# A two-layer network with a gated mixing layer: another order of the mixing steps, and down products held back by two blocks

## The chip, the cores and the metric

The kernel runs on one core of a Trainium2 chip. The core has a matrix engine (TensorE, PE in the profile, with its weight loads PEld), a vector engine (VectorE, DVE), an activation engine (ScalarE, ACT), a general engine (GpSimd, POOL) and a queue engine that issues most of the transfers (SyncE, SP). Each engine works through its own stream of instructions; semaphores between the streams carry the dependences. The metric is the device time of one execution in microseconds (us); less is better.

## The reference

The input is 256 tokens of 1024 features. The network has a gated delta-rule layer, a feed-forward, a sliding-window attention layer, a second feed-forward, then a mixing layer and a layer of selected experts. The change touches the two feed-forwards and the mixing layer:

```
def conv_gated_mlp(hn, w_up, conv_w, conv_b, w_down):
    u = causal_dwconv(hn @ w_up, conv_w, conv_b)
    gate, val = jnp.split(u, 2, axis=-1)
    return (jax.nn.silu(gate) * val) @ w_down
```

```
h = rmsnorm_2(x, norm1_g[l])
z = h @ w_in[l]
conv_in = z[..., :o_conv]                                  # 2048 wide
q, k, v = ...                                              # 16 query heads, 4 key and value heads
gates = jax.nn.sigmoid(z[..., o_v:]).reshape(b, s, 2, d)   # 2 x 1024
conv_out = conformer_conv(conv_in, ...)
attn_out = windowed_gqa(q, k, v, attn_sink[l]) @ attn_w_o[l]
merged = gates[:, :, 0, :] * conv_out + gates[:, :, 1, :] * attn_out
x = x + merged @ w_out[l]
```

`conformer_conv` gates one half of its input with the sigmoid of the other, runs a 31-tap depthwise convolution over the tokens, a layer norm over the 1024 channels, SiLU, and a pointwise product. The feed-forward is 2816 wide on each side; its convolution has 3 taps.

## The kernel before

Activations lie transposed: 128 features on the partitions, 256 tokens along the free axis, so 1024 features are eight blocks. Every large product is made of three matmuls (`mm3`, L237 to L241): a float32 weight is split into a high part `wh` (cast on ScalarE, L232) and a low remainder `wl` (VectorE or GpSimd, L223), the activation likewise into `xh` and `xl`, and wh·xh + wh·xl + wl·xh is summed in PSUM. `proj` (L247) makes 256 output columns from 1024 inputs with 48 such matmuls and two weight pieces of half a megabyte; `kouter` (L262) adds the share of two input blocks to all eight output blocks, also 48 matmuls and two pieces. Pieces go through pools of four buffers.

PSUM is eight banks in three pools: `pp` (2), `pm` (2) and `pa` (4). A product that adds over a whole stage (`acc4`) holds all four `pa` banks. While `self.wide` is set, projections go round over `pp` and `pa`.

**Feed-forward** (`ffn`, L749): a loop over 11 blocks of 256 columns. Each makes two projections (gate and value), evicts and convolves them on VectorE and ScalarE, multiplies, and splits the result into `gh` (L788) and `gl` (L789). `lower` adds the block's down product to the four `pa` banks. It is held back in `pend`, so that block i's down product is written behind block i+1's projections; the last one follows the one before it.

**Mixing** (`mix`, L1290): steps are functions, and the string `MIX` (L75) says in which order they are written. A step is a letter and a number:
- `c0..c3` convolution input: two projections, sigmoid, product, into the padded tile `upad`;
- `d0..d15` convolution: block m = i // 2, first or second half of the 31 taps. ScalarE makes the first tap (L1326), VectorE adds each further one in a dependent step (L1329); the running sum of two blocks at a time lies in one `pm` bank (`taps`), the last tap goes to the tile `conv`;
- `q`, `k` projections for the heads; `S0..S7`, `P0..P7` scores and values of one key head and one block of queries;
- `g0..g7` gate projections (L1345), of which 0 to 3 are the first branch's (convolution) and 4 to 7 the second's (attention); `s` their sigmoid;
- `o0..o3` the attention's output product (transposes at L1218, low halves at L1224, then `kouter` into the `pa` banks); `a0` multiplies it with the second branch's gates (L1355);
- `L0` the layer norm's mean (column sums of `conv`, L319; a row over all partitions, L299) and subtraction (L1365); `N0` its variance, scaling and SiLU (L1373 to L1384); `R0` a scaling of the residual;
- `w0..w3` pointwise products with the gates, `e0..e3` the layer's output product.

The string is the order in which the program is written. A scheduler then places the instructions of each engine, before the kernel runs, by a timeline of its own; it keeps the order in which tiles of a pool are handed out. So a tile of `pm` is given to a later step only when an earlier one has released it: `taps` holds one of the two banks until the convolution is over, and column sums, rows and the transposes of `o` share the other.

Of the kernel before, what the change touches and what calls it, by code (L numbers as in the profile page):

```python
# [11 lines left out]
F32R = mybir.dt.float32r  # L12
# [9 lines left out]
P = 128  # L22
T = 256
# [15 lines left out]
def shape_constants():  # L39
# [7 lines left out]
    for k in range(DB):  # L47
# [24 lines left out]

GDN = "d0 d1 d2 z0 p0 d3 p1 p2 p3 b0 v1 v0 z1 i0 s1 v2 s0 z2 i2 o1 v3 o0 s2 z3 s3 o2 o3"
SWA = "q2 q0 S0 S1 P0 q1 S3 S2 P1 S4 P3 o0 P2 P4 q3 S5 o1 S7 P7 S6 P5 P6 o2 o3"
MIX = ("c0 q0 d0 d1 q1 d2 c1 d3 k0 d4 S0 S1 d5 P0 q2 d6 P1 S2 c2 d7 S3 P2 d8 q3 P3 d9 S4 c3 d10 S5 P4 d11 g4 S6 d12 "  # L75
       "P5 g5 S7 d13 P6 g6 d14 P7 g7 d15 s8 s12 o0 o1 o2 o3 a0 g0 g1 L0 g2 g3 N0 R0 s0 s4 w0 w1 e0 w2 e1 w3 e2 e3")
PEER = " ".join([f"q{i} k{i}" for i in range(8)] + [f"T{i}" for i in range(8)] + [f"u{i}" for i in range(32)])


# [8 lines left out]
class Net:  # L88
# [21 lines left out]
    def t(self, pool, shape, tag, dt=F32, **kw):  # L110
        return pool.tile(shape, dt, tag=tag, name=self.nm(tag), **kw)
# [637 lines left out]
    def ffn(self, l, nxt, hook=None, each=None):  # L749
        nc, tc, I, t = self.nc, self.tc, self.I, self.t  # L750
        up, down = I["ffn_w_up"][l], I["ffn_w_down"][l]
        cw, cb = self.fconv[l], self.fbias[l]
        self.stage = "ffn"
        x = self.input(self.v["ffn_norm_w"][:, 8 * l : 8 * l + 8])
        with tc.tile_pool(name=f"ffn{l}", bufs=2) as fp:
            _, rrow = self.rstd(self.hT, fp, "sq")
            acc = None
            pend = []
            self.wide, self.nwide = True, NW[0]

            def lower(i, gh, gl):
                nonlocal acc
                if acc is None:
                    acc = self.acc4()
                self.kouter(acc, down, (2 * i, 2 * i + 1), [(gh[:, kk, :], gl[:, kk, :]) for kk in range(2)],
                            i == 0, i == 10)

            for i in range(11):
                if hook:
                    hook(i)  # L770
                cv = []
                for part in range(2):
                    ps = self.proj(up, part * 2816 + 256 * i, x)
                    nc.vector.tensor_mul(ps, ps, self.bc(rrow))
                    o = t(fp, [P, 2, T], f"cv{part}")
                    for m in range(2):
                        blk = part * 22 + 2 * i + m
                        w = [cw[j][:, blk : blk + 1] for j in range(3)]
                        nc.scalar.activation(o[:, m, :], ps[:, m, :], AF.Identity, scale=w[2], bias=cb[:, blk : blk + 1])
                        for d in range(1, 3):  # L780
                            nc.vector.scalar_tensor_tensor(o[:, m, d:], ps[:, m, : T - d], w[2 - d], o[:, m, d:],
                                                           op0=ALU.mult, op1=ALU.add)
                    cv.append(o)
                nc.scalar.activation(cv[0], cv[0], AF.Silu)
                nc.vector.tensor_mul(cv[0], cv[0], cv[1])
                gh = t(fp, [P, 2, T], "gh", F32R, bufs=3)
                gl = t(fp, [P, 2, T], "gl", F32R, bufs=3)
                nc.scalar.copy(gh, cv[0])  # L788
                nc.vector.tensor_sub(gl, cv[0], gh.bitcast(F32))  # L789
                pend.append((i, gh, gl))  # L790
                if len(pend) > 1:
                    lower(*pend.pop(0))
            lower(*pend.pop(0))
            self.residual(acc, nxt, None, each)


# [493 lines left out]
    def mix(self):  # L1290
# [5 lines left out]
        with tc.tile_pool(name="mix", bufs=1, reuse_waits="tile") as mp, \  # L1296
# [106 lines left out]
            def resnorm(_):  # L1403

                row = self.rrow(r1, ap, "sc256")
                for k in range(DB):
# [3 lines left out]
            self.wide, self.nwide = True, NW[3]  # L1410
            self.play(MIX, c=conv_in, d=conv, k=lambda _: self.heads_kv(w_in, 3072, 3328, x, rrow, rcol, kT, v),
                      q=lambda i: self.heads_q(w_in, 2048, x, rrow, qT, i, self.c[:, C_SL : C_SL + DB]), g=gate, s=sig,
# [82 lines left out]
```

## Time and profile before

| | |
|---|---|
| median of three runs | 2007.62 us (2006.73 to 2009.07) |
| the profiled execution | 2006.97 us, of which the span from first to last instruction is 2005.2 us |
| delta-rule layer | 0 to 324 us |
| first feed-forward | 324 to 510 us |
| window attention | 510 to 609 us |
| second feed-forward | 609 to 803 us |
| mixing, to its last output product | 803 to 1071 us |
| experts and end | to 2005.2 us |
| HBM read, written | 298.60 MB, 4.74 MB: 151 GB/s over the span |
| main transfer queue | 49.2% of the 16 DMA engines' time |

Times in the profile are microseconds from the first instruction, durations in the group rows are nanoseconds. "L1329" is a line of the kernel; `pm<-upad,colsdw,pm` names the tile written and those read. What stands in brackets is the time that the engine sat idle ahead of the row, and what ended it. The granted clock is TensorE's, as a share of full speed.

### The profile page before, as it was taken

The numbers are of one execution on the slowest core, as the hardware profiler recorded it, in microseconds if no ns is written. First come the engines' busy times: TensorE is split into PE (matmuls) and PEld (weight loads), VectorE is DVE, ScalarE is ACT, GpSimd is POOL, SyncE is SP. The second block draws the span as 40 slices with busy tenths as digits, with TensorE's granted clock in tenths as the row PEclk, the third lists the DMA queues.
The fourth block names the chain that finished last, engine by engine and source line by source line (L and its number), as shares of the span: only waits on it lengthen the run. The fifth ranks groups of instructions, "written<-read, shape, count | busy, mean of one in ns | idle before, by whom it ended". The sixth has DMA issues, their size and how long they took to land. (4 is left out here: it accounts for less than half of the span.)

```text
span 2005.2 us, 36808 instructions
## 1 busy us (share of the span) xinstructions
PE 1867.5 (93%) x14537; PEld 1760.0 (88%) x14537; DVE 1464.4 (73%) x2685; ACT 958.3 (48%) x1419; POOL 709.2 (35%) x325
## 2 busy tenths in 40 slices
PE   7879999999899999999969988799999999999998
PEld 7879999999889999989969978699989978887886
DVE  6786656766536666688854899977999977886555
ACT  5744435555555555556445434234333334344443
POOL 5444343544323444755634445454332300000000
PEclk9989999999899999999979999999999999999999
DMA  6454236566424665433535544456455545445555
GB/s 201 124 146 139 89 100 202 190 191 195 126 83 147 202 191 176 153 121 117 162 102 150 147 128 138 119 159 174 137 147 138 148 147 167 159 160 172 194 194 173
DMA packets 243434, 306.29 MB, mean 153 GB/s; under 512 B 26076, under 2 KB 213821, under 8 KB 243133
## 3 DMA queue, kind: packets, MB, share of 16 engines
q1 hardware_dynamic: 240864, 302.84, 49.2%
q8 instruction: 114, 1.87, 0.4%
q10 hardware_dynamic: 2237, 1.07, 0.2%
q14 instruction: 59, 0.48, 0.1%
q0 software_dynamic: 160, 0.02, 0.0%
HBM read 298.60 MB, written 4.74 MB: 151 GB/s over the span
## 5 line engine op out<-in xcount | busy, mean ns | idle before, releaser
L223 POOL TENSOR_TENSOR wl<-raw,wh 128x1024 fp32r<-128x1024 f32 (+1 forms) x196 | 470.7, 2405 | 555.0 <-ACT wh L232 506.9
L232 ACT CAST wh<-raw 128x1024 fp32r<-128x1024 f32 (+1 forms) x285 | 297.8, 1048 | 322.2 <-issue 108.9
L239 PE MATMUL pa<-xh,wh 128*128 128x256 f32 (+1 forms) x1336 | 388.8, 291 | 26.9 <-ACT wh L981 17.8
L239 PE MATMUL pp<-xh,wh 128*128 128x256 f32 x1392 | 395.5, 284 | 16.6 <-DVE kq L481 9.8
L241 PE MATMUL pp<-xh,wl 128*128 128x256 f32 x1392 | 394.3, 283 | 4.1 <-DVE wl L223 2.6
L241 PE MATMUL pa<-xh,wl 128*128 128x256 f32 (+1 forms) x1336 | 386.8, 291 | 11.0 <-DVE wl L223 7.6
L240 PE MATMUL pp<-xl,wh 128*128 128x256 f32 x1392 | 393.1, 282 | 2.1 <-DVE xl L364 2.1
L240 PE MATMUL pa<-xl,wh 128*128 128x256 f32 (+1 forms) x1336 | 385.3, 289 | 1.6 <-DVE xl L364 1.5
L223 DVE TENSOR_TENSOR wl<-raw,wh 128x1024 fp32r<-128x1024 f32 x233 | 296.8, 1274 | 112.3 <-ACT wh L232 55.8
L223 POOL TENSOR_TENSOR wl<-rt,wh 128x1024 fp32r<-128x1024 f32 x80 | 203.2, 2546 | 272.4 <-ACT wh L981 258.9
L239 PEld LDWEIGHTS pa<-xh,wh 128*128 128x128 f32 (+1 forms) x1336 | 262.3, 197 | 32.2 <-ACT wh L981 21.6
L239 PEld LDWEIGHTS pp<-xh,wh 128*128 128x128 f32 x1392 | 266.9, 192 | 18.8 <-issue 10.2
L241 PEld LDWEIGHTS pa<-xh,wl 128*128 128x128 f32 (+1 forms) x1336 | 262.1, 197 | 13.7 <-DVE wl L223 8.7
L241 PEld LDWEIGHTS pp<-xh,wl 128*128 128x128 f32 x1392 | 266.8, 192 | 6.1 <-DVE wl L223 3.7
L240 PEld LDWEIGHTS pp<-xl,wh 128*128 128x128 f32 x1392 | 267.1, 192 | 2.5 <-DVE xl L364 2.3
L240 PEld LDWEIGHTS pa<-xl,wh 128*128 128x128 f32 (+1 forms) x1336 | 262.1, 196 | 3.0 <-DVE xl L364 1.9
L981 ACT CAST wh<-rt 128x1024 fp32r<-128x1024 f32 x128 | 133.9, 1049 | 223.1 <-DVE rt L978 204.3
L1086 PE MATMUL pa<-wh,rt 128*128 128x512 f32 x512 | 200.9, 394 | 0.0
L1085 PE MATMUL pa<-wl,rt 128*128 128x512 f32 x512 | 200.3, 391 | 0.0
L1076 ACT CAST wh<-raw 128x1024 fp32r<-128x1024 f32 x128 | 134.5, 1051 | 108.6 <-PE pa L1086 97.3
L978 DVE STREAM_TRANSPOSE rt<-raw 128x1024 f32<-128x1024 f32 x128 | 156.3, 1229 | 16.9 <-POOL wl L223 16.6
L1084 PE MATMUL pa<-wh,rt 128*128 128x512 f32 x512 | 161.4, 393 | 1.4 <-ACT rt L1070 1.4
(422 smaller groups left out, 3450.2 us busy)
## 6 DMA issues: line engine op xcount, KB each, us to landing
raw<-in_peer_u_dram SPq DMA_DIRECT2D x512, 128.0 KB
raw<-in_peer_v_dram SPq DMA_DIRECT2D x128, 512.0 KB
raw<-in_ffn_w_up_dram SPq DMA_DIRECT2D x88, 512.0 KB
raw<-in_a_w_in_dram SPq DMA_DIRECT2D x48, 512.0 KB
raw<-in_ffn_w_down_dram SPq DMA_DIRECT2D x44, 512.0 KB
raw<-in_w_in_dram SPq DMA_DIRECT2D x44, 512.0 KB
raw<-in_a_w_out_dram SPq DMA_DIRECT2D x16, 512.0 KB
raw<-in_peer_w_query_dram SPq DMA_DIRECT2D x16, 512.0 KB
```

The costliest lines, as they stand in the source:

```text
L223: (self.nc.vector if order[self.turn % len(order)] == "D" else self.nc.gpsimd).tensor_tensor(out, raw, high, op=ALU.subtract)
L232: nc.scalar.copy(wh, raw)
L239: mm(out, wh, xh, start=start, stop=False, skip_group_check=skip)
L240: mm(out, wh, xl, start=False, stop=False, skip_group_check=skip)
L241: mm(out, wl, xh, start=False, stop=stop, skip_group_check=skip)
L978: nc.vector.transpose(rt, raw)
L981: nc.scalar.copy(uh.rearrange("p f (b e) -> p f b e", b=4), rv)
L1076: nc.scalar.copy(vh, raw)
L1084: nc.tensor.matmul(o, w2[:, 0, i, s], vh[:, c], start=first, stop=False)
L1085: nc.tensor.matmul(o, w2[:, 0, i, s], vl[:, c], start=False, stop=False)
L1086: nc.tensor.matmul(o, w2[:, 1, i, s], vh[:, c], start=False, stop=last)
```

## The change

The string for mixing gets another order, and the feed-forward keeps two blocks' results in `pend` instead of one, with four buffers for `gh` and `gl` instead of three.

```diff
-MIX = ("c0 q0 d0 d1 q1 d2 c1 d3 k0 d4 S0 S1 d5 P0 q2 d6 P1 S2 c2 d7 S3 P2 d8 q3 P3 d9 S4 c3 d10 S5 P4 d11 g4 S6 d12 "
-       "P5 g5 S7 d13 P6 g6 d14 P7 g7 d15 s8 s12 o0 o1 o2 o3 a0 g0 g1 L0 g2 g3 N0 R0 s0 s4 w0 w1 e0 w2 e1 w3 e2 e3")
+MIX = ("c0 q0 d0 q1 d1 k0 d2 c1 d3 S0 d4 S1 q2 d5 P0 d6 c2 S2 d7 P1 d8 S3 q3 d9 c3 d10 P2 S4 d11 P3 d12 S5 d13 "
+       "P4 S6 d14 P5 d15 S7 P6 g4 P7 g5 L0 g6 g7 s8 s12 o0 o1 o2 N0 o3 a0 g0 g1 R0 g2 g3 s0 s4 w0 w1 e0 w2 e1 w3 e2 e3")
...
-                gh = t(fp, [P, 2, T], "gh", F32R, bufs=3)
-                gl = t(fp, [P, 2, T], "gl", F32R, bufs=3)
+                gh = t(fp, [P, 2, T], "gh", F32R, bufs=4)
+                gl = t(fp, [P, 2, T], "gl", F32R, bufs=4)
...
-                if len(pend) > 1:
+                if len(pend) > 2:
                     lower(*pend.pop(0))
-            lower(*pend.pop(0))
+            for p in pend:
+                lower(*p)
```

Behind L792 the changed kernel's lines have a number higher by one. What the scheduler makes of the change is seen in each engine's stream. Three places of it follow, as rows of line, operation, tile written and tiles read, size, and how often the row stands there in succession.

TensorE at the end of the second feed-forward, before: the last row of block 10's value projection (`pp`), then the down product of block 9 (48 matmuls, the first one shown) and that of block 10.

```order
L241 MATMUL pp_9065<-xh_6951,wl_9100 128x256
L239 MATMUL pa_7300<-gh_8932,wh_9142 128x256
...
L241 MATMUL pa_7303<-gh_8932,wl_9150 128x256
L239 MATMUL pa_7300<-gh_9136,wh_9202 128x256
L239 MATMUL pa_7301<-gh_9136,wh_9202 128x256
L239 MATMUL pa_7302<-gh_9136,wh_9202 128x256
```

The same place after: behind the value projection stand the down products of blocks 8 (`gh_8668`), 9 (`gh_8872`) and 10 (`gh_9076`).

```order
L241 MATMUL pp_9005<-xh_6951,wl_9040 128x256
L239 MATMUL pa_7444<-gh_8668,wh_9082 128x256
...
L239 MATMUL pa_7444<-gh_8872,wh_9142 128x256
...
L239 MATMUL pa_7444<-gh_9076,wh_9202 128x256
L240 MATMUL pa_7444<-gl_9077,wh_9202 128x256
L241 MATMUL pa_7444<-gh_9076,wl_9204 128x256
```

Between block 10's projection and its own down product now stand 96 matmuls instead of 48.

VectorE at the end of the convolution, before. `gates` is the eviction of a gate projection, `pm_9333` the running sum, `conv` a block's result.

```order
L223 TENSOR_TENSOR wl_11784<-raw_11780,wh_11782 128x1024
L1329 SCALAR_TENSOR_TENSOR pm_9333<-upad_9329,colsdw_48_207,pm_9333 128x256
L1345 TENSOR_TENSOR gates_9342<-pp_11583,rrow_9327 128x512
L1329 SCALAR_TENSOR_TENSOR pm_9333<-upad_9329,colsdw_48_207,pm_9333 128x256 x5
L1329 SCALAR_TENSOR_TENSOR conv_9332<-upad_9329,colsdw_48_207,pm_9333 128x256
L1362 TENSOR_SCALAR mu_11497<-pm_11498 128x2
L1365 TENSOR_TENSOR conv_9332<-conv_9332,pm_11516 128x1024 x2
```

The same place after, from the eviction of the last gate projection that stands ahead of the mean (g7); the last three steps' rows, of the seventh block, come once more for the eighth where the dots are.

```order
L1346 TENSOR_TENSOR gates_9342<-pa_11049,rrow_9327 128x512
L1330 SCALAR_TENSOR_TENSOR pm_9333<-upad_9329,colsdw_45_201,pm_9333 128x256
L223 TENSOR_TENSOR wl_11205<-raw_11201,wh_11203 128x1024
L1330 SCALAR_TENSOR_TENSOR pm_9333<-upad_9329,colsdw_45_201,pm_9333 128x256
L1330 SCALAR_TENSOR_TENSOR pm_9333<-upad_9329,colsdw_48_207,pm_9333 128x256 x14
L1330 SCALAR_TENSOR_TENSOR conv_9332<-upad_9329,colsdw_48_207,pm_9333 128x256
L1330 SCALAR_TENSOR_TENSOR pm_9333<-upad_9329,colsdw_45_201,pm_9333 128x256 x15
...
L1363 TENSOR_SCALAR mu_10963<-pm_10964 128x2
L1366 TENSOR_TENSOR conv_9332<-conv_9332,pm_10982 128x1024 x2
L1225 TENSOR_TENSOR aol_11123<-pm_11117,aoh_11122 128x512
```

Before, six convolution steps stand between the last gate eviction ahead of the mean (g3) and the mean; after, it is 77 (1 + 1 + 14 + 1, then twice 15 + 14 + 1) behind g7, and the evictions of g0 to g3, the four low halves (`aol`) and the four products with the gates stand behind the mean.

TensorE at the same moments, before: the last row of g3, the column sums over the last block, the row of the mean, the variance's sums and row, a row for the residual, then the first pointwise product.

```order
L241 MATMUL pp_11583<-xh_9260,wl_11618 128x256
L319 MATMUL pm_11498<-ones_85,conv_9332 128x1 x2
L299 MATMUL pm_11516<-c_head_81,mu_11497 128x128 x2
L319 MATMUL pm_11656<-ones_85,sc_1537_11645 128x1 x4
L299 MATMUL pm_11664<-c_head_81,rcol_11661 128x128 x2
L299 MATMUL pm_11693<-c_head_81,r_1241_9314 128x128 x2
L239 MATMUL pp_11714<-upad_11667,wh_11717 128x256
```

After: the last row of g7, the column sums over the last three blocks, the row of the mean, then the transposes and products of o0. Behind o2 come the variance's sums and row, then o3, g0 to g3 and the first pointwise product.

```order
L241 MATMUL pa_11049<-xh_9260,wl_11084 128x256
L319 MATMUL pm_10964<-ones_85,conv_9332 128x1 x6
L299 MATMUL pm_10982<-c_head_81,mu_10963 128x128 x2
L1219 MATMUL pm_11117<-c_head_81,otok_9343 128x128 x4
L239 MATMUL pa_11113<-aoh_11122,wh_11128 128x256
...
L319 MATMUL pm_11335<-ones_85,sc_1500_11324 128x1 x4
L299 MATMUL pm_11343<-c_head_81,rcol_11340 128x128 x2
L1219 MATMUL pm_11372<-c_head_81,otok_9343 128x128 x4
L239 MATMUL pa_11113<-aoh_11377,wh_11383 128x256
...
L239 MATMUL pp_11714<-upad_11346,wh_11717 128x256
```

What moved here are 384 matmuls: o0 to o3 and g0 to g3 stood ahead of the mean's row and now stand behind it. The projections ahead of g4 keep their order among themselves but for k, v, which now come ahead of c1; the scores and values S4 to S7 and P2 to P6 stood between projections (q3, c3 and g4 to g7) and now stand together, ahead of g4.

## Prediction

> **What bounds the kernel now.** I read the page's first rows, then busy time by stage, then the waits of TensorE in the two stages that the change touches, then the timelines of VectorE and TensorE at the end of mixing.
>
> ```profile
> span 2005.2 us, 36808 instructions
> PE 1867.5 (93%) x14537; PEld 1760.0 (88%) x14537; DVE 1464.4 (73%) x2685; ACT 958.3 (48%) x1419; POOL 709.2 (35%) x325
> ```
>
> TensorE is busy 93% of the span, so over the whole program it is the bound. A share says nothing of one stage, hence the table by stage (from:to, length, busy time of PE, PEld, DVE, ACT, POOL, granted clock, DMA share, GB/s):
>
> ```profile
> 324.00:510.00 186.00, 182.72 (x1565) 181.55 (x1564) 122.71 (x173) 101.58 (x134) 80.56 (x34) 0.99 0.61 193
> 609.00:803.00 194.00, 190.23 (x1596) 189.62 (x1596) 125.92 (x179) 108.02 (x145) 81.75 (x35) 0.97 0.57 180
> 825.40:1006.50 181.10, 173.38 (x1439) 167.68 (x1437) 155.35 (x374) 98.11 (x165) 110.94 (x47) 0.97 0.46 147
> 1006.50:1021.00 14.50, 5.29 (x25) 4.64 (x25) 8.57 (x16) 6.65 (x12) 0.69 (x1) 0.55 0.11 37
> 1021.00:1072.50 51.50, 47.48 (x384) 46.99 (x384) 25.14 (x34) 22.67 (x30) 23.98 (x10) 0.93 0.42 127
> ```
>
> The first two rows are the two feed-forwards: TensorE has under 4 us free in each. The third is mixing from its first convolution step to its last: TensorE is busy 173 of 181 us, but VectorE also 155, so there two engines are nearly full. The fourth is the layer norm behind the convolution, where TensorE has next to nothing to do: 14.5 us that the change may be after. The fifth is the pointwise and output products.
>
> ```profile
> 1003.42 2.58 DVE L1329 SCALAR_TENSOR_TENSOR pm<-upad,colsdw,pm 128x256 f32<-128x256 f32 x5
> 1006.04 0.48 DVE L1329 SCALAR_TENSOR_TENSOR conv<-upad,colsdw,pm 128x256 f32<-128x256 f32 x1
> 1007.22 0.16 DVE L1362 TENSOR_SCALAR mu<-pm 128x2 f32<-128x2 f32 x1 [0.70 <-PE pm L319]
> 1008.20 2.35 DVE L1365 TENSOR_TENSOR conv<-conv,pm 128x1024 f32<-128x1024 f32 x2 [0.83 <-PE pm L299]
> ```
>
> The convolution ends on VectorE at 1006.5. Five steps end to end take 2.58 us, so one starts every (2.58 - 0.49) / 4 = 0.523 us. TensorE over the same moments:
>
> ```profile
> 1006.57 0.60 PE L319 MATMUL pm<-ones,conv 128*128 128x1 f32 x4 [3.80 <-DVE conv L1329]
> 1013.04 1.84 PE L319 MATMUL pm<-ones,sc 128*128 128x1 f32 x8 [4.87 <-DVE sc L309]
> 1015.90 1.22 PE L299 MATMUL pm<-c_head,rcol 128*128 128x128 f32 x4 [1.02 <-POOL rcol L329]
> ```
>
> Its column sums (L319) wait for the last step of the convolution: with its own work done, it waits for VectorE.
>
> **The feed-forward edit.** Two instruction streams are the same in content; only the down products move one block later, and the last block's are now behind two others instead of one. The waits of TensorE in the first feed-forward (us in total, times, longest; the second answers with the same two rows), and, below, 3 us pieces at the end of the second (length, PE busy, granted clock, DMA share, GB/s):
>
> ```profile
> PE pa L239 <- ACT gh L788: 1.9, 1, 1.9
> PE pa L240 <- DVE gl L789: 1.4, 1, 1.4
> ...
> 793.00:796.00 3.00, 1.00 (x6) 1.00 0.55 175
> 796.00:799.00 3.00, 3.00 (x17) 0.56 0.55 175
> 799.00:802.00 3.00, 3.00 (x25) 0.87 0.00 0
> ```
>
> TensorE stands 3.3 us for the last block's gh and gl. Behind it the granted clock is 0.56 and 0.87: ((1 - 0.56) + (1 - 0.87)) x 3 / 0.5 = 3.5 us at half clock, 1.7 us lost. One down product of 48 matmuls (5.5 us at the rate below) now covers the chain up to 3.3 us; two cover 10.9 and the chain needs 8.8, so the stall and its half clock go: 5.0 us in each, **10.0 us gained** in both. If the half clock stays (the residual behind it also leaves TensorE idle) it is 6.6. At the front the first down product comes a block later, and the projection there takes its place; TensorE's waits show none at that place, so I cost it at nothing. The fourth pair of gh and gl takes only memory. The DMA rows move with their products, at the same rate of two half-megabyte pieces per 48 matmuls, which the 0.55 to 0.61 DMA share carries now.
>
> **The mixing edit, VectorE's side.** By the order of instructions, VectorE has twelve instructions fewer ahead of the last convolution step: four gate products' evictions (L1345), the four low halves of the attention output (L1224), and the four products with the second branch's gates (L1355). Its groups and waits in the stage (count, busy, mean ns, idle before; then us, times, longest):
>
> ```profile
> L1345 DVE TENSOR_TENSOR gates<-pa,rrow 128x512 f32<-128x512 f32 x6 | 4.1, 686 | 0.1
> L1224 DVE TENSOR_TENSOR aol<-pm,aoh 128x512 fp32r<-128x512 f32 x4 | 2.8, 692 | 2.8 <-ACT aoh L1223 2.8
> L1355 DVE TENSOR_TENSOR gates<-pa,gates 128x512 f32<-128x512 f32 x4 | 2.8, 690 | 0.6 <-PE pa L241 0.6
> L1329 DVE SCALAR_TENSOR_TENSOR pm<-upad,colsdw,pm 128x256 f32<-128x256 f32 x232 | 113.2, 488 | 10.8 <-ACT pm L1326 5.0
> ...
> DVE den L1182 <- ACT es L1176: 4.0, 3, 2.0
> ```
>
> 12 x 0.69 = **8.3 us less**, so the convolution ends at 998.2 on the time axis of before, if VectorE's idle time (181.1 - 155.35 = 25.7 us) stays. It is bounded from both sides. Below: TensorE has the same products ahead of the fourth gate product (g7) as before, and after it VectorE still has 77 convolution steps:
>
> ```profile
> 952.86 0.69 DVE L1345 TENSOR_TENSOR gates<-pa,rrow 128x512 f32<-128x512 f32 x1
> 850.00:860.00 10.00, 8.46 (x74) 7.80 (x72) 9.24 (x24) 5.50 (x7) 8.22 (x4) 1.00 0.72 222
> 860.00:870.00 10.00, 8.90 (x48) 8.26 (x49) 6.06 (x24) 4.90 (x20) 0.77 (x1) 0.66 0.21 69
> ```
>
> Before, g7 is evicted at 952.9. The only thin place ahead of it is 850 to 870: 1.5 + 1.1 us idle and (1 - 0.66) x 10 = 3.4 us of clock; q2 now stands between the first scores and their values there, so up to 6 us may go, to 947. Then 77 x 0.523 = 40.3 us: not before 988. Above: P2 to P6 and S4 to S7 now stand together with no projection between them, and each may make VectorE wait for its exponentials; the longest such wait is 2.0 us, five units give 10: not after 1008. I take 998, which lies in the middle of both and comes from the longest sum of rows.
>
> **The mixing edit, TensorE's side.** This is the large term. Before, TensorE has all of o0 to o3 and g0 to g3 behind it when the convolution ends, and 14.5 us later starts w0. After, its queue holds the column sums over the last blocks (x6) directly behind g7, then the row of the mean, and only then o0. It must wait there while VectorE does the 77 steps: some 40 us idle, and what it did before the end now comes behind it:
>
> ```profile
> 1020.00:1030.00 10.00, 6.65 (x35) 6.36 (x36) 5.65 (x12) 4.80 (x9) 0.00 (x0) 0.58 0.00 0
> 1040.00:1050.00 10.00, 10.00 (x88) 10.00 (x87) 2.83 (x4) 4.20 (x4) 5.86 (x3) 1.00 0.59 196
> ```
>
> A dense product takes 10 / 88 = 0.1136 us, so 48 take 5.45. From the last step of the convolution to w0:
> - column sums, mean, subtraction, then the low half for o0 behind the subtraction in VectorE's queue: 1008.20 + 2.35 - 1006.52 + 0.69 = 4.7;
> - o0, o1, o2: 144 x 0.1136 = 16.4;
> - the restart at half clock: from 1020 to 1030 the clock was 0.58, so (1 - 0.58) / 0.5 x 10 = 8.4 us at half, 7.4 of them after TensorE's start at 1021.0: 3.7;
> - the variance: its column sums and row stand side by side in TensorE's queue. At full clock half of 1.84, the wait of 1.02 and half of 1.22: 2.5;
> - o3: 5.45, and about 2.0 ahead of it for its low half, which stands behind two products of the norm (3 x 0.69): 7.5;
> - g0 to g3: 192 x 0.1136 = 21.8. The norm's SiLU work lies beside these.
>
> That is 56.6 us against 14.5: **42.1 us more**. Given back: 35 products took the 9.0 us from 1021 to 1030 where 4.0 are due, and w0 now comes out of a running queue: 5.0 less.
>
> The trace shows some 3.5 us at half clock behind the short stall at 796, but 7.4 behind the long one at 1021, where the products also waited for their inputs; I take the longer, since the new stall is long too. The Trainium skill ("TensorE: Matmul & The Clock Gate", Part 1: The HAM clock gate) says that the gate opens again after one busy window of about 3.4 us. By that page the restart would cost 1.7, an estimate, and the sum would be 2 us lower.
>
> **Sum.** The profiled execution took 2006.97 us (span 2005.2, the rest around it; the median of three runs is 2007.62, 0.65 above). -10.0 - 8.3 + 42.1 - 5.0 = +18.8: **2025.8 us**. From the last output product on, the instruction streams of all engines are the same, so no later stage enters.
>
> **The rivals.**
> 1. *VectorE takes up its idle time (the other side).* Place: c3 to the end of the convolution. If it never waited, only the 0.035 us between dependent steps (240 x 0.035 = 8.4) of its 25.7 us would stay, and the convolution would end 17.3 us sooner, at 981: 2008.5, no change. For it: more convolution is free of other work. Against: g7 plus 40 us says 988. It decides from 983 on: sooner, and the result is not slower by 0.2% (4 us, about what a measurement of this kernel tells from no change). Chance 0.05.
> 2. *TensorE passes the waiting column sums* and runs o0 to g3 under the convolution. Then only -8.3 and -10.0 are left: 1988.7. Nothing in the profile shows a matmul that overtakes a waiting one, but at 1002 to 1006 nothing ready stood behind it. Chance 0.04. The Trainium skill (same page, Part 3, The mechanism) holds against it: weight loads may be pulled ahead, matmuls start and end strictly in order. No run here shows more.
> 3. *The bunch of scores and values is worse*: every P waits for its S with TensorE idle and at half clock, and the convolution ends near 1016: 2044. For it: 860 to 870, where the first unit cost that. Against: two score buffers, and convolution steps between. Chance 0.08.
> 4. *The feed-forward gains nothing*, since the residual's idle time takes the stall's place: 2035.8. Chance 0.05.
>
> **How the numbers follow.** The forecast case has the remaining 0.78. Its own bounds are 10 us either way from the end of the convolution, 2 below from the restart, 3.4 above from the feed-forward's clock: 2013.8 to 2039.2. With rival 4 inside, the range 2013 to 2040 leaves out 0.17 (rivals 1, 2 and 3). Faster by over 0.2%: rival 2, 0.04. Within 0.2%: rival 1, 0.05. Slower: 0.91.
>
> **What would show it.** In the new profile: one wait of TensorE's L319 for DVE conv of some 40 us; VectorE busy without a gap under it; the clock at 0.5 when o0 starts; o0 to g3 behind the norm's first row; about 55 us from the last convolution step to the first product with upad; no wait for gh and gl at the end of the feed-forwards, and mixing's start 10 us sooner. It is wrong if the wait at L319 is short, which would mean that VectorE was far ahead or that the column sums don't hold up the queue.

## The result and the profile after

The changed kernel takes 2027.1 us in the median of five runs (2024.5 to 2035.3), the kernel before 2006.9 (2003.2 to 2009.1): a ratio of 1.0105, 95% interval 1.0085 to 1.0126. It is slower by 20.2 us; 18.8 were forecast. The profiled execution of the changed kernel is the longest of its five, 2035.3 us, with a span of 2033.5. First its page, the busy time of the engines:

```profile
span 2033.5 us, 36817 instructions
PE 1870.5 (92%) x14537; PEld 1761.5 (87%) x14537; DVE 1479.1 (73%) x2690; ACT 958.7 (47%) x1418; POOL 696.4 (34%) x320
```

TensorE is as busy as before (1870.5 against 1867.5 us) in a span that is 28 us longer: the loss is mostly waiting (time at a lower clock counts as busy). The table by stage (from:to, length, busy time of PE, PEld, DVE, ACT, POOL, granted clock, DMA share, GB/s) shows the two feed-forwards, the convolution from its first step to its last, the stretch from there to the first pointwise product (w0), and the pointwise and output products:

```profile
326.20:506.00 179.80, 179.80 (x1560) 179.04 (x1559) 120.55 (x174) 103.16 (x136) 78.71 (x34) 1.00 0.64 200
612.30:791.10 178.80, 178.80 (x1541) 178.80 (x1540) 121.31 (x172) 103.92 (x137) 78.56 (x33) 1.00 0.60 189
813.20:986.70 173.50, 130.40 (x1021) 123.92 (x1020) 148.77 (x362) 75.48 (x141) 69.19 (x29) 0.86 0.33 103
986.70:1054.60 67.90, 59.44 (x425) 57.58 (x426) 34.45 (x40) 29.54 (x38) 26.28 (x11) 0.86 0.33 104
1054.60:1106.00 51.40, 50.08 (x429) 49.89 (x428) 24.46 (x34) 27.33 (x37) 27.32 (x11) 1.00 0.56 172
```

The feed-forwards are now full from end to end at full clock. In the convolution TensorE has 43.1 us free where it had 7.7, while VectorE keeps its 24.7 us of idle time (25.7 before). And the fourth stage, 14.5 us before, is 67.9 us long. TensorE's waits and timeline in the third and fourth stage:

```profile
PE pm L319 <- DVE conv L1330: 41.6, 3, 15.3
PE pa L239 <- ACT aoh L1224: 3.0, 3, 1.6
PE pa L241 <- DVE wl L223: 2.5, 1, 2.5
PE pm L299 <- POOL rcol L329: 2.1, 1, 2.1
```

```profile
954.07 1.01 PE L319 MATMUL pm<-ones,conv 128*128 128x1 f32 x4 [10.96 <-DVE conv L1330]
970.41 1.01 PE L319 MATMUL pm<-ones,conv 128*128 128x1 f32 x4 [15.33 <-DVE conv L1330]
986.75 1.02 PE L319 MATMUL pm<-ones,conv 128*128 128x1 f32 x4 [15.33 <-DVE conv L1330]
988.02 1.22 PE L299 MATMUL pm<-c_head,mu 128*128 128x128 f32 x4 [0.25 <-DVE mu L1363]
...
990.77 1.23 PE L239 MATMUL pa<-aoh,wh 128*128 128x256 f32 x4 [0.67 <-ACT aoh L1224]
...
1007.25 0.74 PE L239 MATMUL pa<-aoh,wh 128*128 128x256 f32 x4 [1.63 <-ACT aoh L1224]
1013.39 0.94 PE L319 MATMUL pm<-ones,sc 128*128 128x1 f32 x8
1016.42 1.22 PE L299 MATMUL pm<-c_head,rcol 128*128 128x128 f32 x4 [2.08 <-POOL rcol L329]
...
1019.17 1.23 PE L239 MATMUL pa<-aoh,wh 128*128 128x256 f32 x4 [0.67 <-ACT aoh L1224]
...
1027.83 0.39 PE L239 MATMUL pp<-xh,wh 128*128 128x256 f32 x1 [0.48 <-DVE qT L1385]
...
1042.19 0.39 PE L241 MATMUL pa<-xh,wl 128*128 128x256 f32 x1 [2.55 <-DVE wl L223]
```

TensorE stands at the column sums of block after block, up to 15.3 us for the 30 VectorE steps of one block, 41.6 us in all; behind the last sum come o0 (990.8), o2 (1007.3), the variance (1013.4), o3 (1019.2) and g0 to g3 (1027.8 to 1054.6), as the order of the instructions says. Three of the stops are followed by half clock: the long one, the one of 2.1 us ahead of the variance's row and the one of 2.55 us among the gates. The one of 1.6 us ahead of o2 is not. The stretches at half clock, and one behind o2's stop:

```profile
986.70:996.00 9.30, 8.32 (x36) 7.79 (x37) 3.81 (x5) 1.70 (x3) 0.00 (x0) 0.51 0.00 0
1008.00:1011.00 3.00, 2.94 (x24) 2.94 (x25) 0.70 (x2) 0.39 (x2) 0.64 (x1) 1.00 0.40 129
1016.40:1023.10 6.70, 6.01 (x26) 5.61 (x27) 2.21 (x4) 4.54 (x8) 0.00 (x0) 0.50 0.36 114
1043.70:1047.10 3.40, 3.40 (x19) 3.40 (x18) 0.77 (x1) 1.78 (x2) 0.12 (x1) 0.50 1.02 348
```

Busy time multiplied by one less the clock gives 8.32 x 0.49 = 4.1, 6.01 x 0.50 = 3.0 and 3.40 x 0.50 = 1.7 us lost to the clock at three restarts, 8.8 together.

To compare kernels I use five marks on each profile: the feed-forwards from the norm's sums to the last down product; from the last down product of the second to the end of the last convolution step; from there to w0; from w0 to the sums of the next norm; and the experts behind it. The marks are first and last starts such as these, of before and after:

```profile
L241 PE MATMUL pa<-gh,wl x176: 278/283/415, 636.8 to 802.5; 128*128 128x256 f32 x176
L239 PE MATMUL pp<-upad,wh x64: 278/283/579, 1021.0 to 1059.4; 128*128 128x256 f32 x64
L319 PE MATMUL pm<-ones,rsq x8: 164/250/250, 1083.2 to 1083.9; 128*128 128x1 f32 x8
```

```profile
L241 PE MATMUL pa<-gh,wl x176: 278/283/283, 640.2 to 790.2; 128*128 128x256 f32 x176
L239 PE MATMUL pp<-upad,wh x64: 280/283/283, 1054.6 to 1088.1; 128*128 128x256 f32 x64
L319 PE MATMUL pm<-ones,rsq x8: 166/250/250, 1107.7 to 1108.4; 128*128 128x1 f32 x8
```

| kernel | feed-forwards | to last convolution step | to w0 | to the next norm | experts |
|---|---|---|---|---|---|
| before | 184.4, 185.6 | 204.0 | 14.5 | 62.9 | 921.3 |
| after | 178.8, 177.9 | 196.5 | 67.9 | 53.8 | 925.1 |
| e1, e11 feed-forward edit alone | 178.8, 177.7 | 200.7, 202.2 | 15.4, 15.3 | 63.1, 62.5 | 920.8, 926.1 |
| e2 mixing edit alone | 184.4, 185.6 | 195.1 | 69.1 | 58.0 | 923.4 |
| e3, e10 mean late | 178.8, 177.8 | 202.4, 201.2 | 14.4, 14.4 | 61.3, 62.0 | 923.4, 922.0 |
| e4 sums in pp | 178.8, 177.9 | 193.9 | 48.0 | 57.3 | 923.3 |
| e5 scaling on GpSimd | 179.1, 177.8 | 197.6 | 68.9 | 57.2 | 926.1 |
| e6 mean late, scaling on GpSimd | 178.8, 177.9 | 208.5 | 15.3 | 60.1 | 921.4 |
| e7 o3 and g3 held back | 178.8, 177.9 | 200.2 | 24.4 | 57.5 | 924.2 |
| e8 14 taps fewer | 178.8, 177.9 | 188.6 | 67.3 | 56.9 | 924.3 |
| e9 norm last | 178.8, 177.8 | 193.8 | 60.3 | 62.9 | 920.6 |
| e12 low halves on GpSimd | 178.8, 177.9 | 195.7 | 16.1 | 63.0 | 923.3 |

The last column is a stage with the same instructions everywhere, and it scatters by 5.5 us: part of the excess of the profiled execution after (925.1) may lie there, and not in the change.

### The profile page after: what moved, and what is told of

The parts are those of the page before. It is cut to its first block, busy times and chain, and to the rows that moved or that the text cites. A ratio compares the mean times of both kernels' runs of the same rounds, so it can differ in the third digit from the quotient of the medians.

```text
span 2033.5 us, 36817 instructions
## 1 busy us (share of the span) xinstructions
PE 1870.5 (92%) x14537; PEld 1761.5 (87%) x14537; DVE 1479.1 (73%) x2690; ACT 958.7 (47%) x1418; POOL 696.4 (34%) x320
## 4 chain that ended last, share of the span: by engine, by line
PE 25%; DVE 15%; issue 4%; DMA 3%; SPq 2%; POOL 1%; ACT 1%; DVEq 0%; POOLq 0%
PE pa L1085 6%; PE pa L1087 6%; PE pa L1086 6%; DVE rt L979 4%; DMA raw<-in_peer_u_dram 3%; PE pm L1063 2%; DVE wl L223 2%; SPq L977 2%; PE pa L241 1%; PE pa L239 1%; PE pa L240 1%; DVE ga L1054 1%; DVE gc L1057 1%; PE pp L239 1%; PE pp L240 1%
## 5 line engine op out<-in xcount | busy, mean ns | idle before, releaser
L223 POOL TENSOR_TENSOR wl<-raw,wh 128x1024 fp32r<-128x1024 f32 (+1 forms) x191 | 456.9, 2397 | 600.4 <-ACT wh L232 556.8
L223 POOL TENSOR_TENSOR wl<-rt,wh 128x1024 fp32r<-128x1024 f32 x80 | 202.2, 2534 | 276.9 <-ACT wh L982 257.6
L239 PEld LDWEIGHTS pp<-xh,wh 128*128 128x128 f32 x1376 | 266.2, 193 | 16.1 <-issue 10.2
L982 ACT CAST wh<-rt 128x1024 fp32r<-128x1024 f32 x128 | 134.0, 1049 | 225.2 <-DVE rt L979 193.9
```

The lines of the kernel that those rows point to most:

```text
L223: (self.nc.vector if order[self.turn % len(order)] == "D" else self.nc.gpsimd).tensor_tensor(out, raw, high, op=ALU.subtract)
L239: mm(out, wh, xh, start=start, stop=False, skip_group_check=skip)
L982: nc.scalar.copy(uh.rearrange("p f (b e) -> p f b e", b=4), rv)
```

## The experiments

My theory: the mixing edit costs some 40 us because the mean's sums stand in TensorE's queue ahead of o0 to o3 and g0 to g3, and the feed-forward edit gains some 10. The rivals: the convolution's order or the bunch of scores and values matters; the written order and not a PSUM bank holds o0 back; other engines stretch the work behind the convolution.

**e1 and e2, each edit alone.** e1 has before's `MIX`, e2 before's `ffn`.

> The feed-forward edit alone, the mixing string of before. Theory (each feed-forward loses its stall for gh and gl and the half clock behind it; between the two profiles the way from the norm's sums to the last down product shrank by 5.6 and 7.7 us): 2006.9 - 13.3 = 1993.6 us, 1990 to 1998, no wait of TensorE for gh or gl, and from the last down product to the first pointwise product the 218.5 us of before. Rival (the residual's and the convolution input's idle time take the stall's place): 2003 or more, with a longer way from there to the first pointwise product.

> The mixing string alone, the feed-forwards of before. Theory (the two edits add up): 2027.1 + 13.3 = 2040.4 us, 2035 to 2045; TensorE waits some 42 us for the convolution's last three blocks, and from its last step to the first pointwise product pass 60 to 68 us. Rival (the sooner start of mixing is what makes the stall, because VectorE falls behind): the stall is shorter by 10 us or more and the time below 2032.

e1 took 1991.8 us, a ratio of 0.9918 (0.9898 to 0.9938); e2 2046.2 us, 1.0189 (1.0169 to 1.0209). 0.9918 x 1.0189 = 1.0105, the ratio of both edits together, so they add up. e2's time lies 1 us above its range, and so does its way to w0 (69.1 us; 60 to 68 expected). TensorE's wait for the convolution in e2, then in e1:

```profile
PE pm L319 <- DVE conv L1329: 41.6, 3, 15.3
```

```profile
PE pm L319 <- DVE conv L1330: 5.4, 1, 5.4
```

In e1 no wait for gh or gl is left, and the way to w0 is 216.1 us (218.5 before): nothing takes the stall's place. Both rivals fall.

**e3, the mean late.** The convolution's new order, but the rest of the string as before:

```diff
-"P4 S6 d14 P5 d15 S7 P6 g4 P7 g5 L0 g6 g7 s8 s12 o0 o1 o2 N0 o3 a0 g0 g1 R0 g2 g3 s0 s4 w0 w1 e0 w2 e1 w3 e2 e3"
+"P4 S6 d14 P5 d15 S7 P6 g4 P7 g5 g6 g7 s8 s12 o0 o1 o2 o3 a0 g0 g1 L0 g2 g3 N0 R0 s0 s4 w0 w1 e0 w2 e1 w3 e2 e3"
```

> The changed kernel, but with the mean, the attention's output products and the first branch's gates in the places that they had before; the convolution steps and the bunch of scores and values stay as changed. Theory (the loss lies in the mean's place alone, and the convolution's order is neutral, since VectorE has the same work ahead of its last step): the same as the feed-forward edit alone, 1993.6 us within 5; from the last down product to the last convolution step 204 us as before, to the first pointwise product 14.5 more. Rival A (the convolution's order gains something of its own): below 1988. Rival B (the bunch of scores and values costs): above 2000.

1987.5 us, 0.9895 (0.9873 to 0.9917): 0.5 us on rival A's side of the edge, and so it was run again (e10). The stall is gone, 14.4 us to w0: the whole loss lies in the end of the string.

**e4, the mean's sums in another bank.** The sums and the row of the mean take the two `pp` banks, and the mean is written behind g7:

```diff
-"... g5 L0 g6 g7 s8 ..."
+"... g5 g6 g7 L0 s8 ..."
-                nc.vector.tensor_scalar_mul(mu, self.colsum([cv]), 1.0 / D)
-                row = self.rrow(mu, stay=True)
+                nc.vector.tensor_scalar_mul(mu, self.colsum([cv], None, t(self.pp, [P, 512], "pp")), 1.0 / D)
+                row = self.rrow(mu, stay=True, pr=t(self.pp, [P, 512], "pp"))
```

> The changed kernel, but the mean's column sums and row lie in the two pp banks and not in a pm bank, so that the transposes of o0 to o2 find a pm bank that is free; the mean is written behind g7. Theory (it is the bank that holds o0 to o2 back, since the order in which tiles of a pool are handed out is kept): o0 to o2 run under the convolution, only o3 and g0 to g3 stay behind it; 2027.1 - 16.4 (o0 to o2) - 3 (their restart and waits) + 2.1 (three low halves ahead of the last step again) = 2010 us, 2004 to 2016; the wait for the last convolution steps is some 20 us in place of 42. Rival (the place in the written order decides, not the bank): 2027 within 4 and a wait of 42 us.

2013.7 us, 1.0025 (1.0011 to 1.0039), inside the theory's range. The scheduler now sets o0 to o2 ahead of the last sums, though they are written behind them. TensorE's timeline, from o2's product on:

```profile
951.23 0.74 PE L239 MATMUL pa<-aoh,wh 128*128 128x256 f32 x4 [0.88 <-ACT aoh L1224]
...
967.04 1.01 PE L319 MATMUL pp<-ones,conv 128*128 128x1 f32 x4 [9.54 <-DVE conv L1330]
983.38 1.01 PE L319 MATMUL pp<-ones,conv 128*128 128x1 f32 x4 [15.33 <-DVE conv L1330]
```

The wait is 24.9 us in place of 41.6, and w0 comes 48.0 us behind the convolution. The rival (2027 us, a wait of 42) falls, although the mean's place moved too, behind g6 and g7: it still stands ahead of o0. So it is the bank that held o0 to o2: `taps` keeps one `pm` bank until the convolution ends and the sums the other, so no transpose gets one.

**e5, the residual's scaling on GpSimd.** Between the norm and the gates VectorE scales the residual, eight steps. The groups, before and after:

```profile
L1407 DVE SCALAR_TENSOR_TENSOR hT<-hT,colsv,sc 128x256 f32<-128x256 f32 x8 | 3.3, 481 | 0.0
```

```profile
L1408 DVE SCALAR_TENSOR_TENSOR hT<-hT,colsv,sc 128x256 f32<-128x256 f32 x8 | 11.7, 1524 | 0.0
```

```diff
-                for k in range(DB):
-                    nc.vector.scalar_tensor_tensor(self.hT[:, k, :], self.hT[:, k, :], wf[:, k : k + 1], row,
-                                                   op0=ALU.mult, op1=ALU.mult)
+                for k in range(0, DB, 4):
+                    h = self.hT[:, k : k + 4, :]
+                    nc.gpsimd.tensor_tensor(h, h, wf[:, k : k + 4].unsqueeze(2).to_broadcast([P, 4, T]), op=ALU.mult)
+                    nc.gpsimd.tensor_tensor(h, h, self.bc(row, 4), op=ALU.mult)
-"... s8 s12 o0 o1 o2 N0 o3 a0 g0 g1 R0 g2 g3 ..."
+"... s8 s12 R0 o0 o1 o2 N0 o3 a0 g0 g1 g2 g3 ..."
```

> The changed kernel, but the residual's scaling goes to GpSimd (two multiplications of half a tile each in place of eight steps on VectorE) and is written right behind the mean. In the changed kernel these eight steps took 11.7 us on VectorE between the norm and the first branch's gates, 0.47 to 2.6 us each, where before they took 3.3 us at 0.48 each. Theory (they hold back the low halves and the evictions that g0 to g3 wait for): g0 to g3 shrink from 26.8 to about 22 us, 2027.1 - 5 = 2022 us, 2019 to 2024. Rival (transfers or ScalarE's high parts hold g0 to g3 back): the 26.8 us stay, 2027 within 2; or GpSimd's own low halves come later and it is 2028 or more.

2040.4 us, 1.0164 (1.0134 to 1.0193): the theory falls, and the time is on the side of the rival's second half (2028 or more). The way to w0 is 68.9 us, no shorter than the change's. g0 to g3 take 25.7 us in place of 26.8 (22 expected); they still wait for a low half, now GpSimd's:

```profile
PE pa L241 <- POOL wl L223: 1.9, 1, 1.9
```

Of the 13 us between the medians, the two profiles show 6 (1.1 ahead of the last convolution step, 1.0 behind it, 3.4 between w0 and the next norm, 1.0 in the experts, 0.5 less elsewhere); the rest is not placed.

**e6, the same scaling in e3.**

> The kernel with the mean in its place of before (the third experiment, 1987.5 us), and the residual's scaling on GpSimd. There the eight steps take 3.3 us on VectorE and stand ahead of the low halves that the first pointwise products wait for (2.4 us by TensorE's waits). Theory: that wait goes, and some of its half clock: 1984.5 us, 1982 to 1986. Rival (nothing to gain, since ScalarE's SiLU sets the pace there, or GpSimd's low halves come later): 1987 or more.

1993.4 us, 0.9926 (0.9897 to 0.9955): the theory falls, and the rival's time holds. The multiplications by the weights need nothing of mixing, so the scheduler put them at the start; behind them in GpSimd's queue a low half (805.0 to 807.4) now stands ahead of the norm's factor. VectorE's wait for that factor, of e6 and then in the timeline of its parent e3:

```profile
DVE rcol L1306 <- POOL rcol L329: 3.5, 1, 3.5
```

```profile
806.46 2.35 DVE L1306 TENSOR_TENSOR rcol<-rcol,r 128x2 f32<-128x2 f32 x1 [0.81 <-POOL rcol L329]
```

Counted from the last down product, the convolution's first step comes 3.9 us later than in e3 and its last one 6.1. The times alone hardly tell the two kernels apart, since e3's came out at 1990.2 us when it was run again (e10).

**e7, two products held back.** e6 with this end of the string:

```diff
+"... g5 g6 g7 s8 s12 o0 o1 o2 g0 g1 g2 L0 o3 a0 N0 g3 R0 s0 s4 w0 ..."
```

> As the run before in this list, but with g0 to g2 ahead of the mean and only o3 and g3 behind it, to cover the norm's 14.5 us. Theory (two products are enough to cover the norm and keep the clock up, and the last convolution step comes 6 x 0.69 = 4.1 us sooner since six steps of VectorE stand behind it): from the last convolution step to the first pointwise product 17 to 20 us in place of 14.5, and 4 to 5 us less of half clock behind it: 1980 us, 1976 to 1984. Rival (what is held back comes on top of the norm, as in the change): 1988 or more.

1995.1 us, 0.9941 (0.9927 to 0.9956). The theory falls and the rival holds: w0 comes 24.4 us behind the convolution (17 to 20 expected, 15.3 in e6), and TensorE now waits 14.4 us ahead of its last step, 5.8 in e6.

```profile
PE pm L319 <- DVE conv L1330: 14.4, 1, 14.4
```

The convolution ends 8.3 us sooner than in e6 (200.2 us; 4.1 expected), w0 comes 9.1 us later behind it, and nothing is gained. TensorE is through with its own products and waits for VectorE ahead of the end, and of the 10.9 us of products held back (96 matmuls) 9.1 come on top behind it.

**e8, fewer taps.** The step d15 leaves out 14 of its 15 taps and makes only the last one, so the output is wrong.

```diff
-                for j in range(16 * h or 1, 16 + 15 * h):
+                for j in range(30 if i == 15 else 16 * h or 1, 16 + 15 * h):
```

> The changed kernel without 14 of the 31 taps of the last channel block (the order of the instructions is otherwise the same). Theory (the stall ends with VectorE's last step, and everything behind hangs on it): 14 x 0.523 = 7.3 us less, 2019.8 us, 2017 to 2022, with the wait for the convolution at 34 us in place of 41.6. Rival (something else would end the wait next, such as the weights of o0): less than 4 us gained.

In the profile the wait is 34.3 us in place of 41.6, the 7.3 us expected, and the convolution ends 7.9 us sooner. The median, 2022.9 us, is only 4.2 lower than the change's and 0.9 above its range, with ratios of 1.0078 (1.0050 to 1.0106) and 1.0105 (1.0085 to 1.0126). The wait settles it; the time by itself, with the scatter of the experts' stage in it, would not have.

**e9, the norm last.** The mean stays; the variance with the SiLU, and the residual's scaling, go behind the gates:

```diff
-"... o0 o1 o2 N0 o3 a0 g0 g1 R0 g2 g3 s0 ..."
+"... o0 o1 o2 o3 a0 g0 g1 g2 g3 N0 R0 s0 ..."
```

> The changed kernel, but with the variance and SiLU of the norm (and the residual's scaling) written behind g3; the mean stays in its new place. Since the residual's scaling on VectorE was not what stretched g0 to g3, theory: it is the norm's own work in the queues of ScalarE (SiLU, copies) and VectorE, ahead of the casts and low halves of the weights that g0 to g3 use, together with the short stops that the variance makes in TensorE's queue and the half clock behind each. Then o0 to o3 take 22 to 25 us in one piece, g0 to g3 22 us, and TensorE is through with g3 some 51 us behind the last convolution step in place of 68; the norm's chain then stands by itself: the first pointwise product at 59 to 61 us, and it starts cold again (5 to 9 us): 2022 to 2028 us, no gain in all. Rival (the weights' buffers and transfers stretch g0 to g3): g0 to g3 take 25 us or more here too, and the time is 2030 or more.

2025.5 us, 1.0096 (1.0076 to 1.0115). One of the groups of g0 to g3 in e9, then in the changed kernel:

```profile
L241 PE MATMUL pa<-xh,wl 128*128 128x256 f32 x32 | 8.8, 276 | 0.0
```

```profile
L241 PE MATMUL pa<-xh,wl 128*128 128x256 f32 x32 | 9.8, 307 | 2.5 <-DVE wl L223 2.5
```

g0 to g3 take 1012.8 to 1034.6, 21.7 us as I had priced them, with no wait. So what stretched them to 26.8 is the work that moved behind them, the norm's and the residual's scaling in the other engines' queues, and not the weights' transfers. Which of the two did it, this run can't say, since both moved. In the changed kernel the low half that ends the wait of 2.5 us stands in VectorE's queue right behind the eight scaling steps; in e5 these steps were gone from there, and g0 to g3 still took 25.7. TensorE is through 53.8 us behind the convolution (51 expected; o0 to o3 took 28.0 and not 22 to 25, their transposes among it), w0 comes at 60.3, and it starts at a lower clock (62.9 to the next norm, as before the change).

**e10 and e11, e3 and e1 again, six executions each.**

> The third experiment's kernel once more, beside the feed-forward edit alone, to tell whether the other order of the convolution, scores and values is worth something of its own. Theory (it is neutral): within 3 us of the feed-forward edit alone. Rival (TensorE's gain): 4 us or more below it, as the medians of the first three rounds had it (1987.5 and 1991.8).

> The feed-forward edit alone once more: 1991 us, 1988 to 1994.

1990.2 us, 0.9915 (0.9901 to 0.9930), and 1993.5 us, 0.9928 (0.9912 to 0.9943). The medians differ by 3.3 us, between the theory's 3 and the rival's 4; in the first runs they differed by 4.2. The intervals overlap both times, so neither pair alone tells the difference from zero. Over all ten executions of each kernel the means differ by 3.1 us with a standard error of 1.2: a small gain of the convolution's own new order is likely, and not settled.

**e12, the low halves.** e3, but the stage in which VectorE takes every third low half begins at the norm's variance (`self.stage = "tail"` stands in `norm` and not in `center`).

> The third experiment's kernel, but GpSimd keeps all low halves of the weights until the norm's variance, where before VectorE takes every third one from the mean's steps on: three of them, 5.0 us on VectorE, stand ahead of the last convolution step in the third experiment's profile. Theory (VectorE sets the convolution's end): 4 to 5 us less than the third experiment's kernel beside it. Rival (GpSimd with 2.4 us for each then holds TensorE back, or TensorE's own work ends no sooner): within 2 us of it.

1987.5 us, 0.9911 (0.9895 to 0.9927). Ahead of the last convolution step VectorE has one low half in place of three (e10, then e12):

```profile
L223 DVE TENSOR_TENSOR wl<-raw,wh x3: 1215/1218/2520, 967.4 to 987.5; 128x1024 fp32r<-128x1024 f32 x3
```

```profile
L223 DVE TENSOR_TENSOR wl<-raw,wh x1: 1226/1226/1226, 982.5 to 982.5; 128x1024 fp32r<-128x1024 f32 x1
```

and the convolution ends 5.5 us sooner, but TensorE, no longer waiting for it, has its own work to finish. The median is 2.7 us lower than e10's, between the theory (4 to 5) and the rival (within 2), and the intervals overlap: not settled. e12 and e3 are the fastest kernels here, some 1% below before and 2% below the change.

## Why the prediction was right

Its sum of +18.8 us stands against +20.2 in the medians, inside the range. By its terms, on the profiles:

- **Feed-forwards: -10.0 predicted.** Measured 184.4 to 178.8 and 185.6 to 177.9, -13.3; with the stage between them and the scatter ahead, mixing starts 12.3 us sooner. The mechanism (one more down product covers the chain to gh and gl) held; the size was low by 3, which no row here places.
- **The end of the convolution: -8.3.** 204.0 to 196.5, -7.5; 195.1, 193.9 and 193.8 in e2, e4 and e9. VectorE's idle time stayed at 24.7 us, as the forecast case assumed. Rival 1 falls.
- **From there to w0: 56.6.** 67.9, the term that was mis-sized. The mean took 4.1 (4.7 priced), o0 to o2 22.6 (16.4 + 3.7), the variance 4.0 (2.5), o3 10.4 (7.5), g0 to g3 26.8 (21.8). I priced one restart at half clock, 3.7 us; there were three, 8.8. I left out the transposes, some 0.6 us for each of o0 to o3 at full clock. And "The norm's SiLU work lies beside these" was wrong: e9 shows that this work and the residual's scaling, which I did not price, in the queues that make the weights' high and low halves, hold g0 to g3 back by 5 us.
- **The start of w0: -5.0.** 62.9 to 53.8, -9.1 in this profile; -4.9 in e2.
- **Nothing behind it.** 921.3 and 925.1, inside the scatter of that stage.

That the sum came within 1.4 us of the medians is in part luck. The profiled execution, the longest of five, is 28.3 us above the one before, 9.5 more than the sum: +11.3 to w0, +0.8 at the convolution's end and +1.0 ahead of mixing, against -3.3 and -4.1, and +3.8 of scatter in the experts. The median execution is 8.2 us shorter than this one, and no profile shows where. Each edit alone was further off than the sum: e2 took 38 us more than before (28.8 forecast: -8.3 + 42.1 - 5.0), e1 and e11 some 17 and 14 us less (10.0 forecast), and the two errors have opposite signs. The mechanism is not luck: the wait of 41.6 us for the convolution (some 40 forecast, though it came in three pieces and not in one), the products that run behind the mean, and the loss and the gain of the two edits are what was forecast. TensorE did not pass the waiting sums (rival 2), the bunch of scores and values did not delay the convolution (rival 3), and the feed-forward kept its gain (rival 4). The Trainium skill's figure for a restart ("TensorE: Matmul & The Clock Gate", Part 1: The HAM clock gate: one busy window of about 3.4 us) fits the third restart: the clock fell at 1043.7 and was full again at 1047.1. The second ran at 0.50 for 6.7 us, and the first, with 0.9 us of stops in it, at 0.51 for 9.3. What I took, 7.4 us at half, was nearer to these two.

## What to carry to other kernels

Before a step that waits is moved forward in an in-order queue, ask what ready work stands behind it, and which bank or buffer the waiting step and its neighbours hold: here one tile of PSUM decided that 16 us of ready products could not go ahead. Work moved behind a wait can cost more than its own length, since it then meets other work in every queue that feeds it: 384 matmuls, 43.6 us at the dense rate, stood in a stretch of 67.9. A stop can be paid twice, once as idle time and once as half clock: those of 2.1 and 2.55 us were, the one of 1.6 was not. Work held back to cover a latency is no gain where its engine then waits ahead of that latency: in e7 TensorE's wait for the convolution grew from 5.8 to 14.4 us.

## What the runs showed that was not expected

The same VectorE step took 0.48 us or up to 2.6, depending on GpSimd. The residual's scaling reads and writes SBUF; before, with GpSimd idle, all eight took 0.48. After, GpSimd was making low halves of 2.4 to 2.6 us each:

```profile
1028.53 4.94 POOL L223 TENSOR_TENSOR wl<-raw,wh 128x1024 fp32r<-128x1024 f32 x2 [12.16 <-ACT wh L232]
1034.80 2.60 POOL L223 TENSOR_TENSOR wl<-raw,wh 128x1024 fp32r<-128x1024 f32 x1 [1.33 <-ACT wh L232]
1037.67 2.65 POOL L223 TENSOR_TENSOR wl<-raw,wh 128x1024 fp32r<-128x1024 f32 x1 [0.27 <-ACT wh L232]
```

```profile
1028.74 5.01 DVE L1408 SCALAR_TENSOR_TENSOR hT<-hT,colsv,sc 128x256 f32<-128x256 f32 x2
1033.67 0.68 DVE L1385 TENSOR_TENSOR qT<-pp,upad 128x512 fp32r<-128x512 f32 x1
1034.28 6.72 DVE L1408 SCALAR_TENSOR_TENSOR hT<-hT,colsv,sc 128x256 f32<-128x256 f32 x6
1040.92 1.21 DVE L223 TENSOR_TENSOR wl<-raw,wh 128x1024 fp32r<-128x1024 f32 x1
```

Two steps filled 5.0 us beside two low halves (4.9 us). In e9 GpSimd made no low half beside them, and all eight took 3.3 us again. The convolution's steps, which read one of their tiles from PSUM, keep their 0.49 us (0.48 to 0.49 for all of them in the changed kernel) with GpSimd busy 69 of the stage's 173.5 us. The Trainium skill ("SBUF — State Buffer", Who interferes with whom) has the rule: a VectorE step with two inputs in SBUF and a GpSimd instruction that reads SBUF contend for a shared pair of ports under an exclusive lock, and the second to start waits out the other's instruction. The rows agree: the longest step, 2.62 us, is 0.48 and not quite one low half. It is seen the other way round too: GpSimd's 128x2 step of the variance (L329) took 1.75 us beside a low half on VectorE, where before it took 0.69, and with it TensorE's wait for it grew from 1.0 to 2.1 us. What the slow scaling steps cost the total is not settled: the low half behind them (1040.92) ends TensorE's wait of 2.55 us, but in e5, with the steps moved away, other waits (0.7 us for a high half, 1.9 for GpSimd's low half) took its place and w0 came no nearer.
